# Block differences on the score buffers, and the first feature unit's weights, sums and pieces on bytes that are left early

## The chip, the cores and the metric

The kernel runs on one core of one Trainium2 chip. The metric is the device time of one execution in microseconds, as the median over the runs. TensorE (PE) multiplies, VectorE (DVE), ScalarE (ACT) and GpSimd (POOL) work on tiles in the on-chip memory, and SyncE (SP) issues nearly all of the transfers, one after the other from one queue.

## The reference, cut to what matters

One inference step of an encoder layer over 2048 prompt tokens and 32 sample tokens (2080 in all, width 1024). All columns come from one projection of the normalised input `h`:

```python
h = rms_norm(x, norm_g) * (1.0 + scale) + shift
proj = h @ w_in                                  # q, k, v, za, qi, ki, wi, u, bg, cg, zb, ga, gb
score = sum_h wi[t, h] * relu(qi[t, h] . ki[s])  # indexer: each query keeps its 256 best keys
o = softmax over the kept keys (q . k) @ v       # attention
y_conv = conv3(cg * u)                           # the other branch
y = x + gate * ((sigmoid(ga) * a_out + sigmoid(gb) * b_out) @ w_out)
```

## The kernel before, in words

The kernel has four stages: the **token projections** (columns `qi`, `wi`, `ki`, `k`, `v`, tokens on the output's partitions, to 271 us), the **feature projections** (the other columns, features on the partitions, from the first matmul of line 988 on), the attention, and the output projections. This case is about the border between the first two.

**Token stage** (pools `xp`, `wp`, `hp` of lines 508 to 510). `mk_h` (line 632) makes 256 tokens of `h`: PE transposes `x`, DVE scales, ACT and DVE or POOL split the result into a high and a low part, and the fp32 `h` is stored to `h_d` in DRAM (line 649). `chunk` (line 751) multiplies 128 tokens with the 256 to 320 columns of one weight group: 8 row blocks of three matmuls (lines 760 to 762). The second half of the tokens has 42 steps: five pairs of token tiles with four chunks and one `pair_ahead` each (the last pair has two chunks), the split of the third weight group, and 18 chunks of the groups `k` and `v`. The last `mk_h` of all tokens is made in step 14.

**Block differences.** The feature projection is one level of a Strassen-like scheme with seven products, in which the halves of `h` (tokens by rows) are combined. `sums_load` (line 659) loads two row blocks of `h`, columns of both token halves, 352 or 336 wide; `block_sums` (line 664) makes four subtractions on DVE (line 671), in place, and stores both to `t_d` (line 673). There are twelve such pieces, three column chunks of four row pairs. Before, they lie in the four `x` buffers of the pool `xp`; the load of piece 0 is put ahead of step 15, and each piece's differences and stores two steps behind its load; the next load stands right behind these stores. On the SP queue the order is so: load, load, store, store, load, load, and so on.

**Feature stage** (pools `ep`, `hpa`, `wx`, `hpb`, lines 891 to 894). There are 32 units of 256 columns, in three sweeps over them (`PASSES`, line 904) of three, two and two products. `w_load` (line 907) loads a unit's weights (two loads of 512 KB), `w_sums` (line 929) makes four sums on POOL (line 937), of which `s_keep` (line 944) stores two to `s_d` for the last sweep. `w_piece` (line 949) splits one 128x512 operand: ACT makes the high part (line 190), POOL the low one (line 191). `b_piece` (line 965) fetches one piece of the other operand as four loads into the `ev` ring of seven buffers (line 974) and splits each on ACT and DVE. `mm` (line 981) is one step: twelve matmuls (lines 988 to 990). `keep` (line 993) copies a result out and stores it to `u_d` (line 1001). The first unit has nine steps: products 0, 1 and 3, each over three column chunks. Product 0 reads `h_d`, products 1 and 3 read `t_d`.

**What sets the order.** The program is traced in an order of its own (`weave`, line 86, mixes the feature steps with the index steps in proportion to costs written beside each), and a scheduler reorders each engine's and queue's instructions by priority and by a simulated timeline; `keep_in_program_order` pins some. The index steps (line 212) score the keys of a block of 128 queries (PE lines 246 and 247, ACT 248, DVE 250 and 252) into one of two buffers `sc` of 2048 columns, and then bisect for the threshold.

**Bytes.** The feature stage's pools take the bytes of the token stage's. By the tiles' sizes, in the order of the pools: `xp` takes the first 35 KB of each partition, `wp` 41 KB behind it, `hp` 71 KB; `ep` (the `ev` ring) takes the first 9.9 KB, `hpa` (the first two pieces) 22.5 KB, `wx` (weights, sums, split weights) 37 KB, and `hpb` the rest. So `ep` and `hpa` lie on `xp`, and `wx` lies on the end of `xp` and on `wp`.

Of the kernel before, what the change touches and what calls it, by code (L numbers as in the profile page):

```python
# [66 lines left out]

class Env:
# [35 lines left out]
def body(ctx, tc, x_prompt, x_sample, cache_k, cache_v, cache_idx_k, state_conv, c_prompt, c_sample,  # L104
         w_ada, w_g, b_ada, norm_g, w_t, w_f, q_norm_g, k_norm_g, conv_w, w_q, rope, turns, ident_in, rows_in,
# [401 lines left out]
    with ExitStack() as p1:  # L507
        xp = p1.enter_context(tc.tile_pool(name="xp", bufs=1))
        wp = p1.enter_context(tc.tile_pool(name="wp", bufs=1))
        hp = p1.enter_context(tc.tile_pool(name="hp", bufs=1))  # L510

# [60 lines left out]
        def wtiles():  # L572

            turn[0] += 1
            return [wp.tile([P, KT, 320], F32R, name=nm(tg), tag=f"{tg}{turn[0] % 2}") for tg in ("wh", "wl")]
# [45 lines left out]
        def x_norm(j):  # L621

            if j in xraw:
                for (t, n, off), xt in zip(allp[j], xraw[j]):
                    sq = xp.tile([P, D], BF16, name=nm("sq"), tag="sq")
# [33 lines left out]
        def sums_load(ch, kt):  # L659
            xs = halved[ch, kt] = xtile(), xtile()  # L660
            for x, k in zip(xs, (kt, kt + 4)):
                tc.keep_in_program_order(load(*both(x, h_d[k], *CHUNKS[ch])))
# [60 lines left out]
        def norm_stage1(pm, n):  # L723
            sq = xp.tile([P, D], BF16, name=nm("sq"), tag="sq")
            st = xp.tile([P, 8], F32, name=nm("sn"), tag="sn", bufs=4)
# [12 lines left out]
        def tok_steps(tiles, pairs, w0, p0, first):  # L738
# [89 lines left out]
            else:  # L828
                at = 15
                for j in range(12):  # L830
                    ch, kt = j // 4, j % 4
                    steps.insert(at, (0.0, lambda ch=ch, kt=kt: sums_load(ch, kt)))
                    steps.insert(at + 3, (0.1, lambda ch=ch, kt=kt: block_sums(ch, kt)))
                    at += 4
# [55 lines left out]
    with ExitStack() as p2:  # L890
        ep = p2.enter_context(tc.tile_pool(name="ep", bufs=1, reuse_waits="tile"))
        hps = [p2.enter_context(tc.tile_pool(name="hpa", bufs=1, reuse_waits="tile"))]
        wx = p2.enter_context(tc.tile_pool(name="wx", bufs=1, reuse_waits="tile"))
        hps.append(p2.enter_context(tc.tile_pool(name="hpb", bufs=1, reuse_waits="tile")))
# [3 lines left out]
        wraw, wsum, wop, bop = {}, {}, {}, {}  # L898
# [8 lines left out]
        def w_load(n):  # L907
# [15 lines left out]
            for cc in (c, c1):  # L923
                r = wx.tile([P, 2, 512], F32, name=nm("wr"), tag="wr", bufs=2)
                load(r, w_f[cc].rearrange("p (k c) -> p k c", k=2))
                rs += [r[:, 0, :], r[:, 1, :]]
            wraw[n] = dict(zip(("a1", "a2", "b1", "b2"), rs))

# [15 lines left out]
        def s_keep(n):  # L944
            if n < NF:
                for a, key in enumerate(("s1", "s4")):
                    store(s_d[n][:, 512 * a:512 * a + 512], wsum[n][key])

        def w_piece(n, j):
# [6 lines left out]
            hi = wx.tile([P, 512], F32R, name=nm("wo"), tag="wo", bufs=10)  # L956
            lo = wx.tile([P, 512], F32R, name=nm("wo"), tag="wo", bufs=10)
            split(hi, lo, src, eng=G)
# [6 lines left out]
        def b_piece(k, ch):  # L965
# [6 lines left out]
            for kt in range(4):  # L972
                r = ev()
                load(r[:, :tb], src[k0 + kt, :, hf * HT + c0:hf * HT + c0 + tb])
# [99 lines left out]
        def turns_load(hf, ch):  # L1074
# [3 lines left out]
            for a, t in enumerate(turned[ch]):  # L1078
                load(t[:, :tb], turns[a, :, hf * HT + c0:hf * HT + c0 + tb])
# [56 lines left out]
        def unit_steps(n):  # L1136
# [5 lines left out]
            def step(j, ch):  # L1142
# [14 lines left out]
                if j == 0 and ch == 0:  # L1157
                    w_sums(n + 1)
                if j == 1 and ch == (1 if pss == 0 else 0):
                    w_load(n + 2)  # L1160
                if ch == 2:
# [14 lines left out]
        w_load(0)  # L1176
        w_piece(0, 0)
        b_piece(0, 0)
        b_piece(0, 1)
        w_sums(0)  # L1180
# [10 lines left out]
        for ps, blocks in enumerate(([16, 15, 14, 13, 12, 11, 10, 9, 8], [7, 6, 5], [4, 3, 2])):  # L1191
# [7 lines left out]
            weave(main, side, FAST)  # L1199
# [675 lines left out]
def _consts():  # L1875
# [12 lines left out]
    turns = np.stack([np.tile(t.T, (8, 1)) for t in cols[:2]]).astype(np.float32)  # L1888
    heads = np.kron(np.eye(8), np.ones((16, 1)))
    return {"rope": table, "turns": turns, "ident": np.concatenate([np.eye(P), heads], axis=1).astype(np.float32), "rows": rows}  # L1890
# [62 lines left out]
```

## Time and profile before

| | |
|---|---|
| median of three runs | 2875.97 us (2873.57 to 2882.2) |
| the profiled execution | 2868.78 us |
| its span, first to last instruction | 2867.0 us |
| PE busy | 2749.5 us, 96% of the span |
| DVE, ACT, POOL busy | 77%, 53%, 37% |
| mean granted TensorE clock | 0.984 |

The span is read as one line of PE work with holes in it: where PE is at its full clock and always busy, time is set by the number of matmuls, and where it is idle or at a lower granted clock, time is lost. Busy time alone hides the second kind of loss, since a matmul at a lower clock counts as busy for longer; the number of matmuls in a stretch shows it.

### The profile page before, as it was taken

What the parts mean: (1) busy time and instruction counts of PE and PEld (TensorE: products, weight loads), DVE (VectorE), ACT (ScalarE), POOL (GpSimd) and SP (SyncE); (2) the same over time, 40 slices, a digit from 0 to 9 for tenths busy, and PEclk for the clock granted to TensorE, in tenths of its full rate; (3) what the DMA queues carried; (4) which work ended last, traced back from release to release, by engine and by line L of the source; (5) the groups of instructions that cost most, each with busy time, mean ns of one, the idle gap of its engine ahead of it and who ended that gap; (6) DMA issues with size and microseconds to landing.
All of it is one profiled execution on the core that took longest, in us unless ns stands there. A gap on an engine that the chain in (4) does not pass through costs nothing. (4 is left out here: it accounts for less than half of the span.)

```text
span 2867.0 us, 51829 instructions
## 1 busy us (share of the span) xinstructions
PE 2749.5 (96%) x18206; PEld 2642.5 (92%) x18206; DVE 2193.7 (77%) x4549; ACT 1508.4 (53%) x2719; POOL 1049.3 (37%) x1430
## 2 busy tenths in 40 slices
PE   8998699999999989999999999999999999999998
PEld 6997399999999989999999999888999989999998
DVE  6665947477777789788887865888887768887988
ACT  4442635656665674434554432666666655454453
POOL 3331455456455334222342221467554430010100
PEclk9999799999999999999999999999999999999999
DMA  8547754544445476565676766567655459896785
GB/s 290 181 158 248 240 168 167 175 161 171 161 159 169 155 217 220 196 198 182 220 216 219 218 211 209 142 178 203 166 161 150 127 181 346 265 290 223 247 294 158
DMA packets 485841, 576.29 MB, mean 201 GB/s; under 512 B 179506, under 2 KB 375298, under 8 KB 484546
## 3 DMA queue, kind: packets, MB, share of 16 engines
q1 hardware_dynamic: 476706, 556.55, 61.8%
q0 software_dynamic: 4160, 12.06, 1.2%
q10 hardware_dynamic: 4704, 4.26, 0.5%
q8 instruction: 145, 2.38, 0.4%
q14 instruction: 126, 1.03, 0.1%
HBM read 379.83 MB, written 199.22 MB: 202 GB/s over the span
## 5 line engine op out<-in xcount | busy, mean ns | idle before, releaser
L988 PE MATMUL pm<-bh,wo 128*128 128x352 f32 (+1 forms) x2688 | 867.0, 324 | 13.1 <-DVE u L1087 8.4
L989 PE MATMUL pm<-bl,wo 128*128 128x352 f32 (+1 forms) x2688 | 866.3, 322 | 2.2 <-DVE bl L191 2.1
L990 PE MATMUL pm<-bh,wo 128*128 128x352 f32 (+1 forms) x2688 | 864.0, 323 | 0.4 <-POOL wo L191 0.4
L988 PEld LDWEIGHTS pm<-bh,wo 128*128 128x128 f32 x2688 | 508.1, 189 | 21.6 <-DVE u L1087 10.1
L989 PEld LDWEIGHTS pm<-bl,wo 128*128 128x128 f32 x2688 | 509.2, 189 | 9.4 <-DVE bl L191 3.5
L990 PEld LDWEIGHTS pm<-bh,wo 128*128 128x128 f32 x2688 | 507.9, 189 | 4.0 <-POOL wo L191 0.8
L191 POOL TENSOR_TENSOR wo<-wr,wo 128x512 fp32r<-128x512 f32 x160 | 232.2, 1452 | 614.3 <-ACT wo L190 597.2
L252 DVE SCALAR_TENSOR_TENSOR sc<-pi,wi,sc 128x512 f32<-128x512 f32 (+3 forms) x287 | 191.6, 670 | 68.1 <-ACT pi L248 64.2
L248 ACT ACTIVATE pi<-pi 128x512 f32<-128x512 f32 (+3 forms) x328 | 165.5, 517 | 143.3 <-PE pi L247 140.0
L1525 ACT CAST wh<-rw 128x1024 fp32r<-128x1024 f32 x128 | 134.2, 1053 | 167.9 <-PE ps L1700 77.6
L190 ACT CAST th<-pt 128x512 fp32r<-128x512 f32 (+1 forms) x288 | 154.1, 561 | 122.5 <-PE pt L1429 109.9
L1699 PE MATMUL ps<-xh,wh 128*128 128x384 f32 (+1 forms) x672 | 214.3, 321 | 2.0 <-ACT oa L1654 0.8
L1700 PE MATMUL ps<-xl,wh 128*128 128x384 f32 (+1 forms) x672 | 214.4, 320 | 0.0
L191 DVE TENSOR_TENSOR tl<-pt,th 128x512 fp32r<-128x512 f32 (+1 forms) x288 | 183.9, 655 | 37.9 <-ACT th L190 37.1
L1701 PE MATMUL ps<-xh,wl 128*128 128x384 f32 (+1 forms) x672 | 211.6, 320 | 0.5 <-DVE wl L1526 0.5
L1526 DVE TENSOR_TENSOR wl<-rw,wh 128x1024 fp32r<-128x1024 f32 x128 | 155.3, 1220 | 51.8 <-ACT wh L1525 51.8
L1408 ACT ACTIVATE s<-s,sc,rts 128x640 f32<-128x640 f32 (+15 forms) x128 | 166.0, 1298 | 49.6 <-DVE sc L1407 43.5
L1780 POOL DMA_DIRECT2D out_dram<-om x60 | 31.7, 534 | 389.9 <-DVE om L1778 389.9
L190 ACT CAST wo<-wr 128x512 fp32r<-128x512 f32 x160 | 98.3, 616 | 144.3 <-PE pm L989 114.4
L315 ACT ACTIVATE low<-sc,w 32x1056 f32<-32x1056 f32 (+14 forms) x105 | 136.6, 1301 | 62.7 <-DVE w L320 61.8
L1053 DVE TENSOR_TENSOR u<-u,pm 128x352 f32<-128x352 f32 (+1 forms) x240 | 122.2, 510 | 56.6 <-PE pm L990 54.9
L1437 PE MATMUL po<-th,vhi 128*128 128x256 f32 x544 | 158.9, 292 | 5.3 <-ACT th L190 3.0
(324 smaller groups left out, 7226.6 us busy)
## 6 DMA issues: line engine op xcount, KB each, us to landing
u<-u_d SPq DMA_DIRECT2D x128, 520.0 KB, 3.9
wr<-in_w_f_dram SPq DMA_DIRECT2D x96, 512.0 KB, 4.1
rw<-o_d SPq DMA_DIRECT2D x72, 512.0 KB, 5.0
u_d<-ev SPq DMA_DIRECT2D x192, 176.0 KB, 2.2
rw<-in_w_q_dram SPq DMA_DIRECT2D x56, 512.0 KB, 7.5
s_d<-ws SPq DMA_DIRECT2D x64, 256.0 KB, 2.8
wr<-s_d SPq DMA_DIRECT2D x32, 512.0 KB, 4.6
xa_d<-a SPq DMA_DIRECT2D x64, 256.0 KB, 3.4
```

Of the source, the lines that this page charges most:

```text
L190: S.copy(hi, src)
L191: (eng or V).tensor_tensor(lo, src, hi.bitcast(F32), ALU.subtract)
L248: S.activation(pi[:n, :w], pi[:n, :w], AF.Relu)
L252: V.scalar_tensor_tensor(sc[:n, o:o + w], pi[:n, :w], wi[:n, b, h:h + 1], sc[:n, o:o + w], ALU.mult, ALU.add)
L988: T.matmul(ps[:, :tb], wh[:, kt, :], bh[:, kt, :tb], start=(first and kt == 0), stop=False, **more)
L989: T.matmul(ps[:, :tb], wh[:, kt, :], bl[:, kt, :tb], start=False, stop=False, **more)
L990: T.matmul(ps[:, :tb], wl[:, kt, :], bh[:, kt, :tb], start=False, stop=(kt == 3), **more)
L1408: S.activation(sm[:, :L], sm[:, :L], AF.Exp, bias=sc[:, 16 + i:17 + i], scale=r, accum_out=sc[:, 18 + i:19 + i])
L1437: T.matmul(po[:, 0:256], vh_, th[:, pc], start=(j == 0), stop=False)
L1699: T.matmul(ps[:, :tb], wh[:, kt, wc], xh[:, kt, :tb], start=(first and kt == 0), stop=False, **more)
L1700: T.matmul(ps[:, :tb], wh[:, kt, wc], xl[:, kt, :tb], start=False, stop=False, **more)
L1701: T.matmul(ps[:, :tb], wl[:, kt, wc], xh[:, kt, :tb], start=False, stop=(kt == 3), **more)
```

## The change

1. The block differences move from the four `x` buffers to the two score buffers `sc`; each buffer holds both row blocks of one piece. The steps in which they come are given by a list: piece 0 is loaded behind step 1, and at each later entry the next piece is loaded first and the one before it then subtracted and stored.
2. The token stage's weight pool is cut in two (one for odd, one for even turns), and the small statistics tiles `sq` and `sn` go to a pool `xs` behind `hp`. So the bytes behind `xp` belong to the weight buffers of even turns, whose last user is the group `k`.
3. The split weights `wo` (five pairs of buffers, in turn) are divided: one pair stays in `wx`, four go to a new pool `wy`. By the sizes `xp` now takes 32.9 KB, the even weight pool the bytes up to 53.4 KB, the odd one those up to 73.8 KB; `ep` and `hpa` end at 32.4 KB, `wx` at 52.9 KB, and `wy` at 69.3 KB.
4. The first unit's sums are made ahead of its first piece; its three pieces' low parts are made on DVE instead of POOL; the second unit's sums and pieces come one product later in the first unit's steps.
5. The stores of the sums to `s_d` (64 of 256 KB) are issued by POOL instead of SP.
6. The loads of the pieces of products 1 and 3 and of the weights of units 1 and 2 keep their program order on SP.
7. The first unit's nine steps are woven without index steps; these are spread over the 279 others of the first sweep.

(An input's name changes from `turns` to `rots`, for the name is now a counter.)

```diff
+SUMS_AT = (1, 4, 7, 10, 12, 15, 18, 20, 23, 26, 29, 32, 35)
...
-        wp = p1.enter_context(tc.tile_pool(name="wp", bufs=1))
+        wps = [p1.enter_context(tc.tile_pool(name=f"wp{i}", bufs=1)) for i in range(2)]
         hp = p1.enter_context(tc.tile_pool(name="hp", bufs=1))
+        xs = p1.enter_context(tc.tile_pool(name="xs", bufs=1))
...
         def sums_load(ch, kt):
-            xs = halved[ch, kt] = xtile(), xtile()
+            t = ip.tile([P, SEQ], F32, name=nm("hv"), tag="sc", bufs=2)
+            xs = halved[ch, kt] = t[:, 0:D], t[:, D:2 * D]
...
-                at = 15
-                for j in range(12):
-                    ch, kt = j // 4, j % 4
-                    steps.insert(at, (0.0, lambda ch=ch, kt=kt: sums_load(ch, kt)))
-                    steps.insert(at + 3, (0.1, lambda ch=ch, kt=kt: block_sums(ch, kt)))
-                    at += 4
+                at = {}
+                for j in range(13):
+                    at.setdefault(SUMS_AT[j], []).append(j)
+                put = []
+                for n, f in enumerate(steps):
+                    put.append(f)
+                    for j in at.get(n, ()):
+                        if j < 12:
+                            put.append((0.0, lambda c=divmod(j, 4): sums_load(*c)))
+                        if j:
+                            put.append((0.1, lambda c=divmod(j - 1, 4): block_sums(*c)))
+                steps = put
...
+        wy = p2.enter_context(tc.tile_pool(name="wy", bufs=1, reuse_waits="tile"))
...
-                load(r, w_f[cc].rearrange("p (k c) -> p k c", k=2))
+                (in_turn if 0 < n < 3 else load)(r, w_f[cc].rearrange("p (k c) -> p k c", k=2))
...
+        def in_turn(o, i):
+            tc.keep_in_program_order(load(o, i))
...
-                    store(s_d[n][:, 512 * a:512 * a + 512], wsum[n][key])
+                    G.dma_start(s_d[n][:, 512 * a:512 * a + 512], wsum[n][key])
...
-            hi = wx.tile([P, 512], F32R, name=nm("wo"), tag="wo", bufs=10)
-            lo = wx.tile([P, 512], F32R, name=nm("wo"), tag="wo", bufs=10)
-            split(hi, lo, src, eng=G)
+            pool, nb = (wy, 8) if turns[0] % 5 else (wx, 2)
+            turns[0] += 1
+            hi = pool.tile([P, 512], F32R, name=nm("wo"), tag="wo", bufs=nb)
+            lo = pool.tile([P, 512], F32R, name=nm("wo"), tag="wo", bufs=nb)
+            split(hi, lo, src, eng=G if n else V)
...
-                load(r[:, :tb], src[k0 + kt, :, hf * HT + c0:hf * HT + c0 + tb])
+                (in_turn if k in (1, 3) else load)(r[:, :tb], src[k0 + kt, :, hf * HT + c0:hf * HT + c0 + tb])
...
-                if j == 0 and ch == 0:
+                if (j, ch) == ((1, 0) if n == 0 else (0, 0)):
                     w_sums(n + 1)
...
-                if ch == 2:
+                if n == 0:
+                    if j == 1 and ch:
+                        w_piece(1, ch - 1)
+                    elif j == 2 and ch == 1:
+                        w_piece(1, 2)
+                elif ch == 2:
                     w_piece(n + 1, j)
...
         w_load(0)
+        w_sums(0)
         w_piece(0, 0)
         b_piece(0, 0)
         b_piece(0, 1)
-        w_sums(0)
         s_keep(0)
...
-            weave(main, side, FAST)
+            lead = 0 if ps else 3 * len(PASSES[0])
+            weave(main[:lead], [], FAST)
+            weave(main[lead:], side, FAST)
```

More of the change, by code (lines that the diff above doesn't have):

```diff
@@ L104, in body @@
 def body(ctx, tc, x_prompt, x_sample, cache_k, cache_v, cache_idx_k, state_conv, c_prompt, c_sample,
-         w_ada, w_g, b_ada, norm_g, w_t, w_f, q_norm_g, k_norm_g, conv_w, w_q, rope, turns, ident_in, rows_in,
+         w_ada, w_g, b_ada, norm_g, w_t, w_f, q_norm_g, k_norm_g, conv_w, w_q, rope, rots, ident_in, rows_in,
          y_p, y_s, k_p, v_p, ki_p, conv_p, k_s, v_s, ki_s, conv_s):
@@ L574, in wtiles @@
             turn[0] += 1
-            return [wp.tile([P, KT, 320], F32R, name=nm(tg), tag=f"{tg}{turn[0] % 2}") for tg in ("wh", "wl")]
+            return [wps[turn[0] % 2].tile([P, KT, 320], F32R, name=nm(tg), tag=tg) for tg in ("wh", "wl")]
         def start():
@@ L624, in x_norm @@
                 for (t, n, off), xt in zip(allp[j], xraw[j]):
-                    sq = xp.tile([P, D], BF16, name=nm("sq"), tag="sq")
+                    sq = xs.tile([P, D], BF16, name=nm("sq"), tag="sq")
                     st = xp.tile([P, 4], F32, name=nm("st"), tag="st", bufs=4)
@@ L723, in norm_stage1 @@
         def norm_stage1(pm, n):
-            sq = xp.tile([P, D], BF16, name=nm("sq"), tag="sq")
-            st = xp.tile([P, 8], F32, name=nm("sn"), tag="sn", bufs=4)
+            sq = xs.tile([P, D], BF16, name=nm("sq"), tag="sq")
+            st = xs.tile([P, 8], F32, name=nm("sn"), tag="sn", bufs=4)
             for h in range(2):
@@ L896, in body @@
         pad(hps[1], "hpb")
-        wraw, wsum, wop, bop = {}, {}, {}, {}
+        wraw, wsum, wop, bop, turns = {}, {}, {}, {}, [0]
         def ev():
@@ L1078, in turns_load @@
             for a, t in enumerate(turned[ch]):
-                load(t[:, :tb], turns[a, :, hf * HT + c0:hf * HT + c0 + tb])
+                load(t[:, :tb], rots[a, :, hf * HT + c0:hf * HT + c0 + tb])
         def query(ct, f, hf, ch, uu, ps, second):
@@ L1887, in _consts @@
     table = np.concatenate([table, np.zeros((17 * P - NTOK, 48), np.float32)]).reshape(17, P, 48).transpose(1, 0, 2).reshape(P, 17 * 48)
-    turns = np.stack([np.tile(t.T, (8, 1)) for t in cols[:2]]).astype(np.float32)
+    rots = np.stack([np.tile(t.T, (8, 1)) for t in cols[:2]]).astype(np.float32)
     heads = np.kron(np.eye(8), np.ones((16, 1)))
-    return {"rope": table, "turns": turns, "ident": np.concatenate([np.eye(P), heads], axis=1).astype(np.float32), "rows": rows}
+    return {"rope": table, "rots": rots, "ident": np.concatenate([np.eye(P), heads], axis=1).astype(np.float32), "rows": rows}
 def _chunks(w):
```

## The prediction, on record before the result

> **What bounds the kernel now.** I read the page first: its slices of busy time and granted clock.
>
> ```profile
> PE   8998699999999989999999999999999999999998
> PEclk9999799999999999999999999999999999999999
> ```
>
> PE is busy in nearly every slice at the full clock, so time is PE work plus holes. The one deep hole after the start is the fifth slice (287 to 358 us). The timeline of PE shows what lies around it: the last matmul of the token stage and the first of the feature stage.
>
> ```profile
> 270.99 0.28 PE L762 MATMUL pm<-wh,hlo 128*32 128x256 f32 x1
> ...
> 318.41 0.32 PE L988 MATMUL pm<-bh,wo 128*128 128x352 f32 x1
> ```
>
> I then cut the time into stretches (PE, PEld, DVE, ACT and POOL busy, with the number of instructions; granted clock, DMA share, GB/s):
>
> ```profile
> 155.00:207.00 52.00, 50.84 (x370) 48.51 (x369) 33.42 (x113) 19.22 (x56) 22.00 (x43) 1.00 0.45 147
> 207.00:271.00 64.00, 61.84 (x524) 60.01 (x522) 38.66 (x148) 19.17 (x77) 14.39 (x26) 1.00 0.73 231
> 271.00:310.00 39.00, 20.73 (x69) 7.79 (x66) 23.84 (x49) 13.82 (x34) 0.00 (x0) 0.63 0.73 226
> 310.00:318.40 8.40, 4.47 (x12) 1.88 (x11) 6.89 (x16) 7.30 (x15) 3.94 (x8) 0.88 0.93 326
> 318.40:360.00 41.60, 28.53 (x106) 21.37 (x105) 41.04 (x74) 32.47 (x70) 25.12 (x16) 0.71 0.76 242
> 400.00:440.00 40.00, 40.00 (x250) 39.51 (x249) 10.89 (x26) 20.42 (x35) 20.13 (x21) 1.00 0.54 186
> ```
>
> At full pace PE does 250 matmuls in 40 us, 0.160 us each (last row). From 271 to 360 us it does 69 + 12 + 106 = 187, worth 187 x 0.160 = 29.9 us, in 89.0 us: **59.1 us are lost**, part as idle time (35 us) and the rest at a granted clock of 0.63 to 0.88. POOL does nothing until 310 us: no weights have come.
>
> The timeline of SP says why:
>
> ```profile
> 299.32 2.86 SPq L673 DMA_DIRECT2D t_d<-x  x2
> 302.23 1.28 SPq L662 DMA_DIRECT2D x<-h_d  x2
> ...
> 307.42 2.60 SPq L673 DMA_DIRECT2D t_d<-x  x2
> 310.07 1.09 SPq L925 DMA_DIRECT2D wr<-in_w_f_dram  x2
> 312.38 3.17 SPq L974 DMA_DIRECT2D ev<-h_d  x7
> ```
>
> The feature stage's first weights (line 925) and pieces (line 974) are issued right behind the last store of the block differences. Both lie on bytes of the pool `xp`, whose `x` buffers the differences still use; that no weight was loaded at 271 us, though its bytes hold none of these buffers, says that the release goes by whole pools. And the twelve differences are slow because load, subtraction and store follow each other:
>
> ```profile
> L662 SPq DMA_DIRECT2D x<-h_d x24: 553/617/1064, 207.5 to 302.9; - x24
> L671 DVE TENSOR_TENSOR x<-x,x x24: 485/519/528, 214.4 to 308.4; 128x352 f32<-128x352 f32 x16, 128x336 f32<-128x336 f32 x8
> x<-h_d SPq DMA_DIRECT2D x16, 352.0 KB, 4.8
> t_d<-x SPq DMA_DIRECT2D x16, 352.0 KB, 2.9
> ```
>
> From the first load (207.5) to the last store (310.0) are 102.5 us, 8.5 us a piece, against 4 x 0.52 = 2.1 us on DVE.
>
> **The change part by part.**
>
> *Differences on `sc`, one load ahead.* Now load j+1 stands ahead of the stores of piece j, and the twelve pieces lie behind steps 1 to 35 of 42. The second half of the tokens runs from about 155 to 271 us, 2.8 us a step, so the last stores should fall near 155 + 36 x 2.8 = 255 us. No `x` buffer is held by them, and `xp` is free by about 230 us, with its last weight split. That ends the wait above. What is late next is the stream of pieces (below).
>
> What it costs the token stage: of twelve pieces in 95 us, 52/95 x 12 = 6.6 fall into 155 to 207 us, where none is now. DVE there rises from 33.4 by 6.6 x 2.1 = 13.9 to 47.3 of 52 us, and the transfers from 147 GB/s by 6.6 x 4 x 0.36 MB / 52 us = 183 to 330, as much as the highest stretch above (326). Each piece's stores also wait at the head of SP for DVE, with the stores of `h`, the loads of `x` and the stores of `qi` queued behind them, and `mk_h` waits for those. What SP waited before these stores:
>
> ```profile
> SPq L673 <- DMA x<-h_d: 12.2, 8, 3.1
> SPq L673 <- DVE x L671: 11.2, 11, 2.4
> SPq L673 <- DVE sc L252: 10.0, 5, 2.3
> ```
>
> 33.4 us over 24 stores, 2.8 us a piece. Bounds: nothing, to 6.6 x 2.8 = 18 us. The nearest row is the stretch from 207 to 271: eight pieces ran beside the matmuls and PE lost 64.0 - 61.8 = 2.2 us. I take 4 us, twice that, for the fuller engines; a gain is not excluded, since that stretch gets lighter, but at most its 2.2 us.
>
> *Weights, sums and pieces ahead.* By the sizes `wx` lies on bytes whose last reader is the group `k`, and `k` ends nine chunks ahead of the end (24 matmuls each at 64/524 = 0.122 us: 26 us, so at 245 us). From there 26 us remain for a load, four sums and a split:
>
> ```profile
> wr<-in_w_f_dram SPq DMA_DIRECT2D x96, 512.0 KB, 4.1
> L937 POOL TENSOR_TENSOR ws<-wr x32: 1268/1298/5012, 315.8 to 940.8; 128x512 f32<-128x512 f32 x32
> L191 DVE TENSOR_TENSOR ql<-pt,qh 128x512 fp32r<-128x512 f32 x2 | 1.3, 670 | 0.0
> ```
>
> 4.1 + 4 x 1.3 + 2 = 11 us: covered. The first two pieces of product 0 lie in `hpa` on `xp` and are also ready. So the first feature matmul comes at about 271 us plus the slip, 47 us earlier, and two steps (24 x 0.160 = 3.8 us) have all they need. The three low parts on DVE cost 3 x 0.67 = 2.0 us there, on an engine that then has only the splits to do; without that cover, 2.0 us.
>
> *The stream of pieces.* The other seven pieces lie in `hpb`, on bytes of the last weights and of `h`, and can only be split after the last token matmul. They are 28 loads; seven can wait in the ring, 21 of about 0.177 MB are still to come, 3.7 MB, and the second unit's weights, 1.05 MB. The prices:
>
> ```profile
> ev<-t_d SPq DMA_DIRECT2D x32, 176.0 KB, 3.7
> L190 ACT CAST bh<-ev 128x352 fp32r<-128x352 f32 x24 | 10.8, 479 | 2.6 <-DMA ev<-t_d 2.6
> L191 DVE TENSOR_TENSOR bl<-ev,bh 128x352 fp32r<-128x352 f32 x24 | 19.8, 849 | 0.0
> SPq L974 <- DVE bl L191: 11.5, 11, 2.6
> ```
>
> 4.75 MB take 15 us at 326 GB/s and 20 us at 242; with nine stores of results among them (1.6 MB) 26 us. The first unit's 108 matmuls need 17.3 us. ACT (28 x 0.48 = 13 us) and DVE (28 x 0.85 = 24 us at most; now it shares its time with index work) run beside. So PE is short by 0 to 9 us. The loads pinned in order wait on SP for a free buffer (last row: 1 us each); behind them stand the results' stores and the index loads, and PE waits for neither soon. I take 8 us, the upper part: the last piece needs its landing and split after the stream.
>
> *The displaced index work.* Many of the 187 matmuls were index work, done in the hole for nothing; I counted them at full pace. Their DVE work now falls into the first sweep. DVE has room there (10.9 of 40 us busy in the last stretch), and what PE waited for it from 318 to 1100 us is small:
>
> ```profile
> PE pi L246 <- DVE sc L252: 10.2, 9, 2.0
> PE pm L988 <- ACT ev L1000: 2.6, 2, 2.0
> PE pm L990 <- POOL wo L191: 0.4, 1, 0.4
> ```
>
> 279 steps instead of 288 carry it, 3% more dense: 0 to 6 us, I take 2.
>
> *Stores by POOL.* SP loses 64 issues of 0.32 us; the results' stores come out sooner, which can save at most the 2.6 us above. POOL gets 64 issues. The nearest rows are its stores at the end, its loads of the same size, the stores as they are, how long a unit lasts, and what POOL waits for in the sweep:
>
> ```profile
> L1780 POOL DMA_DIRECT2D out_dram<-om x60: 532/534/556, 2523.0 to 2854.2; - x60
> x<-in_w_g_dram POOLq DMA_DIRECT2D x16, 256.0 KB, 6.0
> L947 SPq DMA_DIRECT2D s_d<-ws x64: 319/320/788, 317.1 to 947.3; - x64
> L1001 SPq DMA_DIRECT2D u_d<-ev x288: 319/320/1650, 356.2 to 1019.8; - x144
> POOL wo L191 <- ACT wo L190: 151.7, 44, 12.3
> POOL ws L937 <- DMA s_d<-ws: 7.3, 9, 1.0
> s_d<-ws SPq DMA_DIRECT2D x64, 256.0 KB, 2.8
> ```
>
> A unit lasts (1019.8 - 356.2) / 32 = 20.7 us, in which POOL gives 1.07 us to issues and has 151.7/32 = 4.7 us of waiting for ACT to cover them. I take nothing; with no cover, 34 us.
>
> *Sum.* 59.1 - 4 - 8 - 2 = 45 us off the profiled execution's 2868.8 us (span 2867.0 and 1.8 around it): 2824. That execution is 7.2 us below the median 2876.0, below all three runs. I take the difference off the median: **2831 us**. The case's own range is from 59 + 2.2 + 2.6 = 64 us gained (2812) to 59.1 - 18 - 9 - 6 = 26 (2850).
>
> **Rivals.**
>
> *A. Only the slide.* The early bytes don't help, since the scheduler or a pool's release puts the feature stage's loads behind the token stage. Then what began at 310 us begins at 271: 39 us, less the 69 matmuls (11 us) that PE did in that time, less the 4 us slip: 24 us, **2852**. For it: releases go by pools, and I can't see the addresses. Against it: an index load of the feature stage is issued 42 us ahead of the border, so the scheduler does reach forward:
>
> ```profile
> 229.21 0.37 SPq L230 DMA_DIRECT2D qd<-qi_d  x1
> ```
>
> *B. The token stage pays more.* If each of the twelve pieces costs PE its 2.8 us of SP, 34 us instead of 4: 15 us gained, **2861**. For it: 330 GB/s and 91% of DVE in 155 to 207. Against it: the 2.2 us for eight pieces.
>
> *C. POOL's stores starve: slower.* Place: the reuse of the four `ws` buffers. A unit's first sum waits until the store of an earlier one has landed. If a store by POOL lands 6.0 instead of 2.8 us after its issue and the sums, the pieces and PE all wait for it, 31 units lose 3.2 us, 99 us in all: 45 - 99 = 54 us slower, **2930**. It decides from 45/31 = 1.45 us a unit. Against it: POOL's wait for these stores is 7.3 us in all, and its low parts are a product ahead of their use, so that PE waited 0.4 us for them.
> The Trainium skill's page "SBUF — State Buffer" (section "SBUF: two separate sides") speaks for this rival: a transfer that GpSimd issues has its descriptors written by GpSimd's own cores, and while VectorE runs an operation that holds both of its ports they can't be written; it advises another queue. By that rule the landing could be longer than 6.0 us. No store by POOL beside index work is in this trace to show it.
>
> *D. It doesn't do what it says.* If the differences still end near 310 us, held by the two buffers or by SP, nothing is gained: **2874**. Against it: at 8 us from load to load, a piece's load has landed (4.8 us) and its buffer's last store too (2.9 us).
>
> **How the numbers follow.** The forecast gets 0.70, A 0.14, B 0.06, C 0.04, D 0.06. Range: 2814 to 2856; it holds most of the forecast and A, and leaves out B, C, D and the tails. A measurement here can tell 0.3%, 8.6 us. Faster by more: forecast, A and nearly all of B, 0.89. Within: D, 0.06. Slower: C and the rest of B, 0.05.
>
> **What would show it.** Right: the last store to `t_d` before 262 us; the first weights loaded between 240 and 260; POOL busy with sums before 271; the first feature matmul within 2 us of the last token matmul; from there nine steps in about 25 us; the last token matmul by 276. Wrong: weights issued at the token stage's end (A); idle PE between 155 and 215 (B); POOL's sums waiting for `s_d`, PE for `wo` (C); a store to `t_d` after the last token matmul (D).

## The result, and the profile after

The changed kernel takes 2846.97 us (median of four runs, 2845.15 to 2851.99) against 2879.09 us for the kernel before in the same comparison (median of four, 2873.57 to 2882.94): a ratio of 0.9893, 95% interval 0.987 to 0.9916. That is 32 us gained where 45 were forecast, inside the range and of the right sign. The profiled execution took 2846.73 us, its span 2844.9.

First the page's slices of PE and of its granted clock, now with no deep hole in the fifth slice:

```profile
PE   8999899999999899999999999999999999999998
PEclk9999899999999999999999999999999999999999
```

The timeline of PE at the border, the last two matmuls of the token stage and the first of the feature stage:

```profile
278.57 0.28 PE L766 MATMUL pm<-wl,hhi 128*32 128x256 f32 x1
278.69 0.28 PE L767 MATMUL pm<-wh,hlo 128*32 128x256 f32 x1
278.80 0.32 PE L1005 MATMUL pm<-bh,wo 128*128 128x352 f32 x1
```

So the feature stage follows at once, 39.6 us earlier than before (318.41), and the token stage ends 7.7 us later (270.99 before). The stretches show what each side costs (columns as before: PE, PEld, DVE, ACT, POOL busy with their counts, granted clock, DMA share, GB/s):

```profile
155.00:207.00 52.00, 47.54 (x344) 44.90 (x343) 39.72 (x121) 17.00 (x48) 21.28 (x38) 1.00 0.80 261
207.00:278.80 71.80, 67.72 (x543) 64.62 (x543) 46.74 (x171) 24.20 (x91) 22.96 (x37) 0.98 0.85 273
278.80:325.60 46.80, 33.70 (x178) 28.84 (x177) 27.41 (x47) 23.49 (x58) 13.81 (x12) 0.82 0.69 219
325.60:365.00 39.40, 39.12 (x249) 37.64 (x248) 17.22 (x36) 20.09 (x43) 29.08 (x32) 1.00 0.60 202
```

In the third row 178 matmuls, worth 178 x 0.160 = 28.5 us at full pace, take 46.8: 18.3 us are lost behind the border, where the prediction allowed 8. By its own accounts, then, 59.1 - 7.7 - 18.3 = 33 us stand to the good at 365 us. To follow the gain from there, I numbered PE's matmuls by their starts (18206 in either trace) and asked when each kernel starts the one of the same number. This table and the later one of its kind give that time less that of before, in us (in a sweep both do the same work, though the order of index and feature matmuls differs a little):

| matmul number (its start before, us) | 2250 (381) | 2500 (425) | 2750 (465) | 7000 (1181) | 12000 (1979) | 18000 (2832) |
|---|---|---|---|---|---|---|
| changed kernel | -34.2 | -36.2 | -30.9 | -25.0 | -21.5 | -19.0 |

From the 2500th to the 7000th matmul, in the first sweep, 11 us of the gain are given back. In the later stages, where the two kernels run the same code, the profiled execution of before is a lucky one: it took 2868.78 us, 10.3 below its median of 2879.09, while the changed kernel's was 0.2 below its own. So the two profiles differ by 22 us and the medians by 32.

### The profile page after: what moved, and what is told of

Read it like the earlier page. It is cut to its first block, busy times and chain, and to the rows that moved or that the text cites. A ratio compares the mean times of both kernels' runs of the same rounds, so it can differ in the third digit from the quotient of the medians.

```text
span 2844.9 us, 51752 instructions
## 1 busy us (share of the span) xinstructions
PE 2741.6 (96%) x18206; PEld 2646.8 (93%) x18206; DVE 2205.9 (78%) x4552; ACT 1506.1 (53%) x2719; POOL 1067.2 (38%) x1491
## 5 line engine op out<-in xcount | busy, mean ns | idle before, releaser
L194 DVE TENSOR_TENSOR tl<-pt,th 128x512 fp32r<-128x512 f32 (+1 forms) x288 | 183.8, 654 | 39.5 <-ACT th L193 38.6
```

The costliest lines, as they stand in the source:

```text
L194: (eng or V).tensor_tensor(lo, src, hi.bitcast(F32), ALU.subtract)
```

## The experiments

Every kernel was timed in three rounds against the kernel before on its chip. A ratio is to that run of before.

### Item 1 alone: the differences early, and nothing else

The kernel before, with the differences on `sc` at the steps of the list; stores on SP, one weight pool, index work everywhere.

```diff
+SUMS_AT = (1, 4, 7, 10, 12, 15, 18, 20, 23, 26, 29, 32, 35)
...
-            xs = halved[ch, kt] = xtile(), xtile()
+            t = ip.tile([P, SEQ], F32, name=nm("hv"), tag="sc", bufs=2)
+            xs = halved[ch, kt] = t[:, 0:D], t[:, D:2 * D]
```

> The kernel before with the first part of the change alone (differences on the score buffers, one load ahead, in the new steps). Account by the border: the pool of the x buffers comes free some 30 us earlier, but the weights' bytes still belong to the last token weights, so the first weights are issued at the last token matmul and the first feature matmul comes 6 to 10 us behind it. Gain 18 to 26 us, ratio to before 0.991 to 0.994. If the early bytes carry the gain: under 9 us, ratio over 0.997. If they carry nothing: 32 us, ratio 0.989.

Measured: 2838.5 us (2835.46 to 2839.68), ratio 0.9868, interval 0.9851 to 0.9884. The token stage's last matmul starts at 277.2 us, the first weights are loaded at 284.0, and the first feature matmul comes at 289.7, 11 us later than in the changed kernel. And yet this part alone gains 37 us, not less than the whole change. Items 2 to 7 together return nothing here. Either they are worth nothing, or one of them pays and another takes it away. The next runs are for that.

### The changed kernel without the early bytes, and without the steps free of index work

Two kernels, each with one part undone. In the first, one weight pool as before and no `wy` (items 2 and 3):

```diff
-            pool, nb = (wy, 8) if turns[0] % 5 else (wx, 2)
-            turns[0] += 1
+            pool, nb = wx, 10
```

> The changed kernel with the weight pool in one again and all split weights in one pool (no early bytes for weights, sums and first pieces of the weights). If the early weights matter: first weights issued at the last token matmul, first feature matmul 6 to 10 us behind it, 6 to 12 us slower than the changed kernel, ratio to before 0.992 to 0.994. If the stream of pieces sets the time of the first unit anyway: within 3 us of the changed kernel, ratio 0.988 to 0.991.

Measured: 2853.06 us (2849.07 to 2854.53), ratio 0.9917 (0.9901 to 0.9934). The first weights are issued at 280.40 us, the first feature matmul comes at 286.8. In the second, index work is woven into the first unit too in the program's order (item 7):

```diff
-            weave(main[:lead], [], FAST)
-            weave(main[lead:], side, FAST)
+            weave(main, side, FAST)
```

> The changed kernel with index steps woven into the first unit as well. If index work is what slows the first unit (its subtractions on DVE before the splits): 5 to 10 us slower, ratio 0.991 to 0.993, and the stretch behind the border loses more than 18 us. If index work only fills what PE waits for there: same or up to 5 us faster, ratio 0.9875 to 0.9895.

Measured: 2852.43 us (2849.39 to 2855.33), ratio 0.992 (0.9904 to 0.9937). Each part seems worth 5 to 6 us by the medians, less than such intervals surely tell apart. So these parts do not lose; something else in the change must. Items 4 and 6 have no run of their own. And item 7 changes less than its words say: in the changed kernel's trace 24 index matmuls, all of the block of sample queries, still stand among the first unit's 108 feature matmuls, and 30 do in this run. The scheduler brings them forward.

### The sums' stores back on SP

```diff
-                    G.dma_start(s_d[n][:, 512 * a:512 * a + 512], wsum[n][key])
+                    store(s_d[n][:, 512 * a:512 * a + 512], wsum[n][key])
```

> The changed kernel with the 64 stores of the sums on SP again. My account gives POOL's issues nothing and SP's relief at most 3 us: ratio to before 0.988 to 0.9905. If stores issued by POOL starve, as rival C has it, this is faster than the changed kernel by more than 5 us: ratio under 0.987. If SP's relief is a real part of the gain: slower by 5 us or more, ratio over 0.991.

Measured: 2840.5 us (2838.55 to 2841.72), ratio 0.9876 (0.9859 to 0.9892), 6.5 us quicker than the changed kernel. Item 5, which the prediction costed at nothing, seems to cost something, though the two intervals overlap. The other way round, item 1 alone with these stores issued by POOL (the same line, the other way):

```diff
-                    store(s_d[n][:, 512 * a:512 * a + 512], wsum[n][key])
+                    G.dma_start(s_d[n][:, 512 * a:512 * a + 512], wsum[n][key])
```

> The first part of the change (differences on the score buffers) and the stores of the sums by POOL, nothing else. If the stores by POOL cost what separates the changed kernel from the one with these stores on SP (2847 against 2840 us): 4 to 8 us slower than the first part alone, ratio to before 0.988 to 0.990, lost in the first sweep and not at the border. If that separation was chance: within 2 us of the first part alone, ratio 0.986 to 0.9875.

Measured: 2852.25 us (2845.96 to 2855.2), ratio 0.992 (0.9901 to 0.9938): 13.75 us slower than item 1 alone. And the changed kernel once more, beside it on the same chip, with nothing edited:

> The changed kernel once more, on the chip of its three variants. If the whole change is worth less than its first part alone, its ratio to before stays above 0.988, and above that of the variants with the stores of the sums on SP. If the difference was that of two chips, it comes to 0.986 to 0.988.

Measured: 2848.12 us (2843.25 to 2852.19), ratio 0.9907 (0.9885 to 0.9928): the first result stands.

### The second unit's weights behind all pieces

Behind the border POOL made the second unit's sums while DVE split the last pieces. Here these weights are loaded later (stores on SP):

```diff
-        w_load(1)
         for ch in range(3):
             b_piece(3, ch)
+        w_load(1)
```

> The changed kernel with the stores of the sums on SP, and the second unit's weights loaded behind all pieces instead of ahead of the last three. If the first unit's splits are slow because POOL makes the second unit's sums beside them (1.18 us a split where 0.49 is usual) and PE then waits 6 us: the splits of the last pieces come back to 0.5 to 0.7 us, PE's wait near 303 us falls under 2 us, 3 to 6 us faster, ratio 0.9855 to 0.9865. If the transfers set the time: the last pieces come 3 us sooner but the weights later, same within 2 us, ratio 0.987 to 0.988.

Measured: 2830.92 us (2828.28 to 2833.99), ratio 0.9846 (0.9827 to 0.9864). This is 9.6 us quicker by the medians than with the old order (2840.5, the run with the stores on SP above, one line away; the ends of the intervals overlap a little), and the quickest version with the whole computation. What happened behind the border shows most sharply in the changed kernel, which differs from this run in two lines, the moved one and the sums' stores by POOL. Its timelines of DVE, POOL and PE (start, duration, and in brackets the idle time before and who ended it):

```profile
302.10 4.32 DVE L194 TENSOR_TENSOR bl<-ev,bh 128x352 fp32r<-128x352 f32 x1
```

```profile
302.31 1.28 POOL L952 TENSOR_TENSOR ws<-wr,ws 128x512 f32<-128x512 f32 x1
303.54 2.48 POOL L194 TENSOR_TENSOR wo<-ws,wo 128x512 fp32r<-128x512 f32 x2
305.96 0.56 POOL L962 DMA_DIRECT2D s_d<-ws  x1
```

```profile
308.70 0.50 PE L249 MATMUL pi<-kiS,qh 128*32 128x352 f32 x1 [5.94 <-DVE sc L253]
```

One split of half a microsecond lasts 4.32 us, as long as POOL's sum and two low parts run on end, and is over 0.4 us after them. DVE's queue stands behind it, and PE waits 5.94 us for an index step of DVE. The splits from 270 to 345 us by tile (min, median and max ns), first in the changed kernel, then with its stores on SP, then with the weights last too:

```profile
L194 DVE TENSOR_TENSOR bl<-ev,bh x28: 484/512/4315, 283.9 to 311.0; 128x352 fp32r<-128x352 f32 x16, 128x336 fp32r<-128x336 f32 x12
```

```profile
L194 DVE TENSOR_TENSOR bl<-ev,bh x28: 488/514/1614, 284.5 to 311.4; 128x352 fp32r<-128x352 f32 x16, 128x336 fp32r<-128x336 f32 x12
```

```profile
L194 DVE TENSOR_TENSOR bl<-ev,bh x28: 487/508/524, 283.6 to 302.3; 128x352 fp32r<-128x352 f32 x16, 128x336 fp32r<-128x336 f32 x12
```

The same 28 splits are done 8.7 us earlier than in the changed kernel, and none of them is long. In that kernel four take 1.07 to 4.32 us, all beside tensor work of POOL; the other 24 have none beside them and take at most 0.52. With the stores on SP and the old order no single split lasts so long, but six in a row take 6.55 us, since the first of them take turns with POOL's operations (up to 1.61 us each), and PE's wait there is 4.09 us:

```profile
301.84 6.55 DVE L194 TENSOR_TENSOR bl<-ev,bh 128x352 fp32r<-128x352 f32 x6
```

Then the stretches, the changed kernel first and this one second:

```profile
302.00:330.00 28.00, 22.06 (x123) 20.68 (x122) 13.35 (x21) 10.78 (x27) 12.47 (x12) 0.82 0.57 181
330.00:365.00 35.00, 34.72 (x221) 33.54 (x221) 15.51 (x33) 17.15 (x37) 24.70 (x28) 1.00 0.59 202
365.00:400.00 35.00, 32.66 (x189) 30.35 (x188) 28.39 (x55) 19.43 (x38) 18.79 (x20) 1.00 0.52 172
```

```profile
302.00:330.00 28.00, 28.00 (x168) 27.27 (x168) 5.16 (x11) 10.26 (x23) 19.36 (x16) 0.94 0.64 210
330.00:365.00 35.00, 35.00 (x224) 33.85 (x222) 16.64 (x43) 21.50 (x45) 22.42 (x22) 1.00 0.66 214
365.00:400.00 35.00, 35.00 (x211) 33.65 (x209) 30.92 (x57) 19.55 (x37) 17.86 (x16) 1.00 0.43 148
```

PE is idle for 8.6 us of 98 in the changed kernel (28.00 - 22.06 and so on), for 7.5 with the stores on SP alone, and for none here.

### The value tiles' stores by POOL

In the changed kernel ACT starts to split the third piece 4.7 us after the token stage's end (283.39 against 278.69), since it first has the last value tiles to evict. Here POOL issues their stores in place of ACT (sums' stores on SP, old order of the weights):

```diff
-                    S.dma_start(v_d[r0:r0 + n, :], vs[:n, :256])
+                    G.dma_start(v_d[r0:r0 + n, :], vs[:n, :256])
```

(and the same for the store to the output)

> The changed kernel with the stores of the sums on SP, and the stores of v issued by POOL instead of ACT. If ACT's own transfer issues hold its queue at the border (the third piece is split 4.7 us after the last token matmul): the split starts within 1.5 us of the last token matmul, the loads of the t pieces by as much earlier, 3 to 5 us faster, ratio 0.9855 to 0.9865. If what ACT waits for is the buffers that the stores free, whoever issues them: same within 2 us, ratio 0.987 to 0.988.

Measured: 2843.55 us (2836.71 to 2848.39), ratio 0.9892 (0.9871 to 0.9912), against 0.9876 with ACT: no gain that can be told, in scattered runs. The token stage's last matmul starts at 279.19 us and ACT's first split of the third piece at 280.47, 1.3 us behind it, as the first account asked; but the time that this account promised with it did not come.

### The whole change with the weights behind all pieces

The changed kernel with the moved line alone, so with the sums' stores by POOL:

```diff
-        w_load(1)
         for ch in range(3):
             b_piece(3, ch)
+        w_load(1)
```

> The whole change as it was made (the sums' stores issued by POOL), with one line moved: the second feature unit's weights are loaded after all pieces. Theory 1 (POOL's issuing of the sums' stores costs by itself, all through the first sweep, whatever the order at the border): slower than the same kernel with these stores on SP (2830.9) by 8 to 14 us, so 2839 to 2845, and the loss grows between the 3500th and the 7000th matmul. Theory 2 (the cost of POOL's stores belongs to the border, where they stand among POOL's sums while DVE splits pieces; with the splits out of the way it is gone): 2829 to 2834. Theory 3 (the moved load doesn't help with these stores): within 3 of the changed kernel's 2847.

Measured: 2845.05 us (2842.64 to 2845.88), ratio 0.9895 (0.9864 to 0.9925): 14.1 us slower than with the stores on SP. The long splits are gone here too (the longest takes 526 ns), so the cost of POOL's stores isn't theirs. The stretch of the whole first sweep, first with the stores on SP, then by POOL:

```profile
365.00:1150.00 785.00, 771.52 (x4701) 753.83 (x4700) 607.64 (x1132) 486.00 (x876) 369.81 (x320) 0.99 0.54 177
```

```profile
365.00:1150.00 785.00, 759.50 (x4593) 738.39 (x4592) 612.32 (x1114) 479.76 (x866) 404.64 (x373) 0.99 0.52 173
```

PE is idle for 25.5 us in place of 13.5, at the same clock, and does 108 matmuls less. (This profile's token stage ended at 283.0 us, the other's at 278.2, but at the 2500th matmul only 2.4 us of that are left.) All three pairs of kernels that differ in who issues these stores differ this way:

| pair | PE idle in 365 to 1150 us, stores on SP / by POOL | matmuls there | medians apart |
|---|---|---|---|
| item 1 alone | 16.8 / 24.7 us | 4667 / 4589 | 13.75 us |
| the change | 20.6 / 23.3 us | 4643 / 4605 | 6.5 us |
| the change, weights last | 13.5 / 25.5 us | 4701 / 4593 | 14.1 us |

In the pair of the change the idle time differs by 2.7 us alone, while 38 matmuls are some 6 us at 0.16 each; the clock there was 1.00 with SP and 0.99 with POOL. Over all 14 profiles of this case, PE is idle there for 12.9 to 20.6 us in the eight whose sums are stored by SP, and for 22.1 to 26.1 in the six whose sums are stored by POOL.

Theory 1 holds for POOL's stores; theory 2 (only the border) is out. Theory 3 half holds: with POOL's stores the moved line brings only 2 to 3 us over the changed kernel's two medians, less than a measurement can tell, though its long splits are gone.

### Item 1 with the weights behind all pieces

The kernel of item 1 alone, with the moved line:

```diff
-        w_load(1)
         for ch in range(3):
             b_piece(3, ch)
+        w_load(1)
```

> The kernel before with item 1 alone (differences early) and the second unit's weights loaded after all pieces; the first unit's weights, sums and pieces wait at the border as before, stores on SP, index work in the first unit too. Theory 1 (items 2 to 4 pay about 10 us once the splits are not beside POOL's sums): 2835 to 2841, slower than 2830.9 by over 4. Theory 2 (the early weights and the steps without index work buy nothing: the pieces set the border's end in either kernel): 2828 to 2834, level with 2830.9.

Measured: 2841.36 us (2835.34 to 2846.19), ratio 0.9888 (0.9855 to 0.9921), against 0.9846 (0.9827 to 0.9864) with items 2 to 4, 6 and 7. That is theory 1's side: 10 us by the medians, though the intervals overlap at their ends. In the profiles it is 3.1 us at the 2500th matmul and 7.1 at the 7000th:

| matmul number | 2250 | 2500 | 2750 | 7000 | 18000 |
|---|---|---|---|---|---|
| item 1 alone | -33.9 | -36.4 | -34.0 | -33.8 | -29.6 |
| item 1, weights last | -36.0 | -38.3 | -35.9 | -37.7 | -33.6 |
| the change, stores on SP | -35.4 | -35.8 | -30.9 | -32.6 | -26.6 |
| the change, stores on SP, weights last | -37.9 | -41.4 | -38.6 | -44.8 | -41.2 |
| the change, weights last | -35.5 | -39.0 | -34.4 | -25.0 | -21.8 |

So items 2 to 4, 6 and 7 together probably pay, once the splits aren't held up by what they bring forward, the second unit's sums. At the border the traces show 3 us of it. What is gained behind the border is less sure: the next run's profile, with the same code in the first sweep as the quickest version, stands at -36.0 at the 7000th matmul where that one has -44.8.

### The value tiles' stores by SP

```diff
-                    S.dma_start(v_d[r0:r0 + n, :], vs[:n, :256])
+                    store(v_d[r0:r0 + n, :], vs[:n, :256])
```

(and the same for the store to the output, on the quickest version)

> The kernel with the sums' stores on SP and the second unit's weights last (2830.9), with the value tiles' stores issued by SP in place of ACT, so that ACT's evictions in the token stage's last 30 us don't stand behind its own issues. Theory 1 (the third piece's late start, 4.7 us after the token stage's end, comes from ACT's queue): the third piece's splits start within 1 us of the token stage's end and the time is 2826 to 2829. Theory 2 (the buffers of pieces or the saturated DMA queues hold the third piece, not ACT): splits start as late as before, time 2829 to 2834; SP's queue gets 66 more issues in the token stage, which could also lengthen that.

Measured: 2833.78 us (2824.66 to 2836.9), ratio 0.9846 (0.9811 to 0.9881): the same as without it. In the changed kernel (first) ACT's copy of a value tile waited for the store of an earlier one to land, and with the stores on SP (second) it does so still:

```profile
281.86 0.37 ACT L782 COPY sm<-pm 128x256 f32<-128x256 f32 x1 [3.45 <-DMA out_dram<-sm]
...
283.39 0.47 ACT L193 CAST bh<-ev 128x336 fp32r<-128x336 f32 x1
```

```profile
281.56 0.36 ACT L782 COPY sm<-pm 32x256 f32<-32x256 f32 x1 [3.40 <-DMA v_d<-sm]
```

By the time it is theory 2. By the trace it lies between the two: ACT splits the third piece from 281.83 us on, 1.6 us behind the last token matmul (280.19), where theory 1 asked for 1 and the changed kernel has 4.7. The wait for a store to land stays, whoever issues it: the small buffers of the value tiles come free late. What this hold of the third piece costs no run shows, since in both runs that shortened it the time stayed.

### No differences at all

On the quickest version, the differences are neither loaded, subtracted nor stored, and the pieces that would read them read the stored `h` itself; the rest of the work is the same, so the numbers computed are others.

```diff
-                        if j < 12:
-                            put.append((0.0, lambda c=divmod(j, 4): sums_load(*c)))
-                        if j:
-                            put.append((0.1, lambda c=divmod(j - 1, 4): block_sums(*c)))
+                        pass
...
-            src, k0, hf = ((h_d, 0, 0), (t_d, 4, 1), (t_d, 0, 0), (t_d, 0, 1), (h_d, 4, 0), (t_d, 4, 0), (h_d, 4, 1))[k]
+            src, k0, hf = ((h_d, 0, 0), (h_d, 4, 1), (h_d, 0, 0), (h_d, 0, 1), (h_d, 4, 0), (h_d, 4, 0), (h_d, 4, 1))[k]
```

> The kernel with the sums' stores on SP and the second unit's weights last (2830.9), without the block differences: neither loaded, subtracted nor stored, and the pieces that would read them read the scores themselves, with the same number of loads and splits (so the numbers computed are others). What stays is what the differences cost in the token stage and at the border. Theory 1 (they lengthen the token stage by the 7.7 us it slipped and hold the stream of pieces by a few more): token stage's end back at about 271 and time 2820 to 2824. Theory 2 (the slip comes from the early weights and pieces, which stay): token end at 276 to 279 and time 2827 to 2833.

Measured: 2817.15 us (2813.48 to 2820.53), ratio 0.9798 (0.9766 to 0.983), 13.8 us below the quickest version. Its stretches before the token stage's end, and ACT at that end:

```profile
155.00:207.00 52.00, 50.68 (x366) 48.14 (x365) 32.61 (x113) 18.71 (x54) 21.20 (x43) 1.00 0.44 144
207.00:268.00 61.00, 61.00 (x519) 59.39 (x519) 30.15 (x129) 22.93 (x86) 16.77 (x30) 1.00 0.53 169
```

```profile
268.52 0.36 ACT L782 COPY sm<-pm 32x256 f32<-32x256 f32 x1 [2.29 <-PE pm L767]
268.79 0.47 ACT L193 CAST bh<-ev 128x336 fp32r<-128x336 f32 x1
```

The token stage's last matmul starts at 268.2 us; in the quickest version it is 278.24. So 10 of the 13.8 us are the differences' price in the token stage, at a DMA share of 0.44 to 0.53 in place of 0.80 to 0.85. The other 4 are behind it: the last copy waits for PE and not for a transfer, and the third piece's first half follows within 0.6 us of the last matmul's start. Theory 1 holds, at the size of 10 rather than 7.7 us and 3 us below its range. The 10 are of two profiles; in all twelve with early differences the stage ends between 274.8 and 283.0 us.

## Why the prediction was right, and where it was off

The forecast's mechanism held. The chain of the differences was what kept PE idle, and once it ends inside the token stage the feature stage follows at once. The sign, the range and the case (not rival A or D) are right. The number alone would not say so: 2846.97 lies 5 us from rival A's 2852 and 16 from the forecast's 2831, and it is the trace, with weights from 259.9 us on and no gap at the border, that decides against A. Three terms of the sum were mis-sized, all to the same side, and one of them went past its bound. That the range held even so is partly luck: its lower end allowed a slip of 18 us, of which 7.7 came. Rival A's kernel is the changed one without the early bytes, and its 2852 us are met by that run (2853.06), but in part by chance: POOL's stores, which that price left out, are in it. Item 1 alone, without them, took 2838.5 us: its first pieces are loaded from 267.7 us on, inside the token stage, so that the border didn't move as it was but grew shorter.

**The hole, 59.1 us.** The first feature matmul came 0.1 us after the last token matmul, as the step asked for (within 2 us). The first sums were to be made ahead of 271 us, and POOL made them from 268 on (timeline of POOL); the weights' loads were issued at 259.9 and 261.9 us, inside the forecast stretch of 240 to 260 but for 2 us.

```profile
268.06 1.28 POOL L952 TENSOR_TENSOR ws<-wr 128x512 f32<-128x512 f32 x1 [10.99 <-DMA wr<-in_w_f_dram]
```

Three signs named there failed. The last store to `t_d` was due before 262 us and came at 277.95, while the token stage was slower and SP's queue stood (nothing was issued from 270.9 to 276.6 us); it still fell ahead of the border. And the nine steps took 41 us and not 25 (the last of their 108 matmuls ends at 320.2). A third, the last token matmul by 276, missed by 2.7.

```profile
277.95 0.71 SPq L678 DMA_DIRECT2D t_d<-hv  x1
284.43 3.60 SPq L942 DMA_DIRECT2D ev<-t_d  x7
```

**The token stage's slip: 4 forecast, 7.7 measured, of bounds 0 to 18.** The value was scaled from the 2.2 us that PE lost beside eight differences in the old second half. The run without differences confirms that row: without any the stage ends at 268.2 us, with the old ones at 270.99. But twelve early ones cost 10 in the quickest version, with the transfers of the stage at a share of 0.80 to 0.85; at its end small buffers come free late. They don't do it by themselves: in the three profiles with item 1 alone the stage ended at 274.8 to 277.2 us, a slip of 3.8 to 6.2, and the first pieces were loaded from 264 us on at the earliest; in the nine that load them from 232 to 236 us on, it ended at 278.0 to 283.0. Which of the early loads add the rest isn't shown. The prediction had worked out the load (330 GB/s and 91% of DVE in the first stretch; 261 GB/s and 39.72 of 52 us, 76%, came of it) and then took a value from a row at a DMA share of 0.73.

**The stream behind the border: 8 forecast with 9 as its upper bound, 18.3 measured.** This is the step that failed. It asked how late the pieces come, from the busy time of the transfers, ACT and DVE, counted the index matmuls at full pace, and said that PE would wait soon for neither the results' stores nor the index loads. The trace has 13.1 of the 18.3 us as idle time of PE (46.80 - 33.70), and the other 5.2 as matmuls at a granted clock of 0.82, for which the sum had no term. What PE waited for from 278 to 330 us (us in total, times, longest):

```profile
PE pi L249 <- DVE sc L253: 8.0, 2, 5.9
PE pi L249 <- ACT qh L193: 1.6, 1, 1.6
PE pi L249 <- DVE sc L255: 1.6, 1, 1.6
PE pm L1005 <- ACT bh L193: 0.9, 1, 0.9
PE pi L250 <- DVE ql L194: 0.8, 1, 0.8
```

A piece's split ended 0.9 us of it; 12.0 us were waits of index matmuls of the sample queries, which stood in PE's order between the feature steps, for index steps of DVE and ACT, which share their queues with the splits. Two waits on those queues stood outside the sum. ACT, in order, held the third piece's split behind value tiles whose buffers waited for their stores (3.45 us), and the loads of the pieces only went on at 284.43 us, 5.7 after the border. And DVE's mean of 849 ns a split, taken as a bound, hid its form: most splits take 0.51 us, and the others wait for POOL's work, one of them through a whole run of it. The old kernel's splits of that time take 486 to 1614 ns with a median of 507, and its long ones lie beside POOL's tensor work too.

The long splits are the smaller part of the term. In the quickest version, which has none, the same 46.8 us hold 197 matmuls, worth 31.5, and lose 15.3; without differences the 46.8 us behind the border (268.3 to 315.1) hold 225 and still lose 10.8. So the case's own bound of 9 was too low even there; what the rest would be without the index matmuls in between, no run shows. The quickest version's row:

```profile
278.80:325.60 46.80, 38.22 (x197) 31.91 (x195) 21.88 (x46) 25.69 (x62) 17.69 (x14) 0.78 0.79 247
```

The Trainium skill's page "SBUF — State Buffer", section "SBUF: two separate sides", says that a VectorE operation with two SBUF inputs and a GpSimd operation that reads SBUF exclude each other, and that whoever comes first keeps the ports for its whole instruction. The trace agrees that they exclude each other; the split of 4.32 us waited for three of POOL's instructions in a row, though, and not for one, while those of the run with the stores on SP took turns with them.

**The displaced index work: 2 forecast.** With the stores on SP, the gain falls by 3.2 us from the 2500th to the 7000th matmul (-35.8 to -32.6). In the quickest version it grows by 3.4 there, so the term can't be told from nothing.

**The stores by POOL: nothing forecast, 6.5 to 14 us measured.** The bound without cover, 34 us, held. Rival C had the right sign for this term and, by the landings, the wrong mechanism. Its landing of 6.0 us didn't come; the DMA issues of the first sweep, with the weights last, show first SP's and then POOL's:

```profile
s_d<-ws SPq DMA_DIRECT2D x52, 256.0 KB, 2.7
```

```profile
s_d<-ws POOLq DMA_DIRECT2D x53, 256.0 KB, 2.6
```

The same section of the Trainium skill, which spoke for the rival, lets POOL's stores wait for descriptors; these landings don't show it. The cover named (4.7 us of waiting for ACT a unit) was an average, and the issues came on top of sums and low parts that run on end:

```profile
L962 POOL DMA_DIRECT2D s_d<-ws x53 | 31.1, 587 | 5.5 <-POOL ws L952 4.2 <-PE pi L250 0.9 <-PE pm L1007 0.3
```

How 31.1 us of issues on POOL become 12 us of idle PE stays open. No one wait of PE carries it. In the first sweep with the weights last, PE waited (us in total, times, longest), first with the stores on SP, then by POOL:

```profile
PE pi L249 <- DVE sc L255: 8.2, 5, 3.2
PE pm L1005 <- ACT ev L1017: 2.1, 2, 1.5
PE pm L1005 <- DVE u L1104: 1.6, 1, 1.6
PE pi L249 <- DVE w L322: 0.8, 1, 0.8
PE pm L1005 <- DVE ev L1015: 0.8, 1, 0.8
```

```profile
PE pi L249 <- DVE sc L255: 7.4, 7, 2.3
PE pm L1005 <- ACT ev L1017: 4.5, 2, 2.3
PE pi L249 <- ACT qh L193: 4.1, 2, 3.2
PE pi L249 <- DVE sc L253: 2.7, 3, 1.2
PE pt L240 <- DVE sc L255: 2.0, 3, 1.3
PE pm L1005 <- DVE u L1104: 2.0, 1, 2.0
PE pm L1005 <- DVE ev L1015: 1.8, 1, 1.8
PE pi L250 <- DVE ql L194: 0.6, 1, 0.6
```

The longer waits are spread over DVE's index steps `sc` (12.1 us where 8.2 were), ACT's splits of queries (4.1, none before) and the evictions (`ev` and `u`: 8.3 us where 4.5 were). That POOL's work holds DVE's two-input operations, as at the border, is a possible cause; no run takes it apart from the mere delay of POOL's own part of the index work.

**The sum.** 59.1 - 7.7 - 18.3 - 3 for the index work and 8 for POOL's stores (the 11 us given back in the first sweep, less these 3) are 22 us on the profiled executions, which differ by 22. So close an agreement is chance: at the 2500th matmul the account has 33 us and the count 36. To take the difference off the median was right in its aim: the profiled execution of before was 10 us on the quick side.

## What to carry to other kernels

A forecast of what comes after a removed wait needs its queue read instruction by instruction: who stands in order ahead of the first step, and whose buffers free it. A mean duration far above the shortest one is not a price but a sign of a wait inside the operation, and work brought forward can land beside the very operations that it excludes. A step that leaves work out of a stretch of the program's order has to be read back in the trace, since a scheduler may bring it in again. When a change has several parts, run its largest alone: here one part gained as much as all together, and two lines (a store's queue and a load's place) were worth another 16 us.

## What the runs showed of the hardware that was not expected

- A DVE split with two SBUF inputs, 0.51 us by itself, took 4.32 us beside three POOL tensor operations that ran on end, and ended 0.4 us after them. In another run such splits took turns with POOL's operations, at up to 1.61 us each. Where POOL did no tensor work beside them, the slowest of 28 took 0.52 us.
- Stores of 256 KB issued by POOL in place of SP cost 6.5 to 14 us over 64 stores in three pairs of kernels, with landings no longer (2.6 and 2.7 us) and with 0.587 us of POOL each.
- With the differences' transfers and subtractions beside them (DMA share 0.80 to 0.85) the token stage's matmuls, which read nothing of these, end 10 us later than without (0.44 to 0.53), and a small result buffer at the stage's end waits 3.4 us for its store to land. Transfers and subtractions were not taken apart.
